# Issuing the cache copies of a hybrid decoder step from ScalarE

## The chip, the core and the metric

The kernel runs on one core of a Trainium2 chip. The core has a matrix engine (TensorE, PE in the profile, with its weight loads as PEld), VectorE (DVE), ScalarE (ACT), GpSimd (POOL) and SyncE (SP), which here only issues transfers. Sixteen DMA engines move data between DRAM and the on-chip memory, and from DRAM to DRAM. The metric is the device time of one launch in microseconds (us).

## What is computed

One decoder layer for a prompt of 512 tokens and for 8 samples of 4 new tokens, all in float32:

```python
h = rms_norm(x, norm_pre)
z = einsum('btd,de->bte', h, w_in)              # 2048 -> 7680: q | k | v | gate | conv a, b | conv gate
att = dilated sliding-window attention, 12 heads # samples read the cache of 2048 old K/V rows
c   = conv module over 512 channels
y = einsum('bte,ed->btd', concat(att * silu(g_att), c * silu(g_conv)), w_out)
x + rms_norm(y, norm_post)
kv_s.append(concatenate([buf, kvs], axis=1)[:, kvs.shape[1]:])   # new cache: old rows moved up by 4
```

The last line matters here. The new cache of each sample is its old cache without the first 4 rows, then the 4 new rows. So 8 times 2044 rows of 12,288 bytes, 201 MB, are copied from DRAM to DRAM unchanged.

## The kernel before

**Projection.** TensorE multiplies w_in with all 544 tokens in 60 projections of 128 output columns, each in four chunks of 512 rows. Both factors are split into a high and a low part of a faster type. A weight chunk is loaded into a tile `raw` (half of a projection's weights, 512 KB, four buffers), ScalarE casts it to `wh` (line 809), GpSimd subtracts to get `wl` (line 810), and then TensorE uses both. A cast is put into the program two chunks ahead of its use, a load two halves ahead of the cast. Projections 0 to 2 run together at the start (`project_first`), and the inverse norms are made at their end; projection 3 is the first of the steady run.

**Beside it.** Attention of the prompt, the samples' attention (which loads the old cache as `kvf` and `kvm`) and the convolution are generators. `tick`, called after each half of two chunks, lets each go on by a step. So every engine's instructions stand in the order in which this one Python program writes them, and `in_order` pins that order.

**Output projection.** From about 957 us on TensorE multiplies with w_out (`owh`, `owl`, `oz`); the samples' rows use `raw` itself (`os`).

**Transfers.** All 635 loads, stores and copies go through `dma` (line 98), which issues from SP. The copies are 176 pieces of 96 rows (1152 KB; 8 of them 336 KB). At its end each `tick` calls `bulk(START + PACE * pe[0])`, which issues copies until the bytes sent by all transfers reach a number that grows with the matmul columns written so far. The framework gives the transfers eight completion semaphores, DMAHW0 to DMAHW7, in turn over the whole program, whichever engine issues them. Before a transfer takes a semaphore again, its issuer waits until the transfer that had it last has landed.

Of the kernel before, what the change touches and what calls it, by code (L numbers as in the profile page):

```python
# [30 lines left out]
ROW = 2 * NH * P  # L31
# [54 lines left out]
def body(tc, xT, xtok, gpost, w_in, w_out, ckv, cconv, relb, vecs, pww, c_oht, c_ohr, c_lmr, c_tm, c_pick,  # L86
         o_y, o_kvp, o_cp, o_cs, o_kvs):
    nc = tc.nc
# [5 lines left out]
    sent = [0]  # L94

    def dma(out, in_):
        sent[0] += 4 * math.prod(out.shape)
        return tc.keep_in_program_order(nc.sync.dma_start(out, in_))
# [222 lines left out]
    def bulk(upto):  # L321
        while d2d_at[0] < len(d2d) and sent[0] < upto:
            b, r, n = d2d[d2d_at[0]]
            d2d_at[0] += 1
            s = ckv[b, NT + r:NT + r + n].rearrange("r c -> (r c)").rearrange("(e x) -> e x", e=16)
            o = o_kvs[b, r:r + n].rearrange("r c -> (r c)").rearrange("(e x) -> e x", e=16)
            dma(o, s)

# [436 lines left out]
    def tick():  # L767
        for s in sorted(sides, key=lambda s: s.rank):
            s.advance(now[0])
            if s.over:  # L770
                sides.remove(s)
        now[0] += 1
        t = now[0]
        flush_late(t)
        bulk(START + PACE * pe[0])
# [370 lines left out]
    for c in range(4):  # L1146
        last = c == 3

        for bs in (((0, 1), (2,), (3,)) if last else ((0, 1), (2, 3))):
# [22 lines left out]
            if last:  # L1172
                if 0 in bs:

                    nc.scalar.activation(stat[:, 0, 8:9], epsc, AF.Sqrt)
                for b in bs:
                    finish(b)
                if 0 in bs:
                    load_xt(2)
                    load_xt(3)  # L1180
                    finish(4)
                if 2 in bs:
                    bulk(1 << 60)
# [116 lines left out]
```

## Time and profile before

| | |
|---|---|
| median of 3 runs | 1174.95 us (1173.05 to 1175.88) |
| the profiled execution | 1170.97 us |
| its span, first to last instruction | 1169.2 us |
| mean granted TensorE clock | 0.99 |
| TensorE busy | 1137.5 us, 97% |
| ScalarE busy | 378.1 us, 32% |
| bytes moved by DMA | 401.92 MB, 344 GB/s over the span |

An engine is busy while it computes; waiting and issuing a transfer do not count. The idle time that matters is that of the engine on which the others wait; that of the rest costs nothing.

### The profile page before, as it was taken

Reading aid. Unit: us, or ns where it says so; the run is one execution under the profiler, and the core shown is the slowest. Engines: PE = TensorE matmul, PEld = TensorE weight load, DVE = VectorE, ACT = ScalarE, POOL = GpSimd, SP = SyncE. Lnnn points to the kernel's source line nnn. Section 1 sums busy time; section 2 is a strip of 40 time slices with the busy share of each in tenths; the row PEclk is TensorE's granted clock in tenths of the full one; section 3 lists DMA queues with packets and bytes.
Section 4 is the critical chain, followed back from the end, with each engine's and each line's share of the span. In section 5 each row is a group of like instructions: output and inputs, shape, how many; then the busy total and the mean of one; then the engine's idle time right before and its main releaser. Section 6 shows DMA issues by size and latency. Waiting matters only on the chain.

```text
span 1169.2 us, 23598 instructions
## 1 busy us (share of the span) xinstructions
PE 1137.5 (97%) x9322; PEld 1029.4 (88%) x9322; DVE 674.0 (58%) x1997; ACT 378.1 (32%) x749; POOL 406.8 (35%) x353
## 2 busy tenths in 40 slices
PE   7899999999999999999999999999999999999996
PEld 7699999999999999999999999899999976776775
DVE  5209899599699988778233576994222243112136
ACT  5433333422123332331334333423222253223241
POOL 5043323344344333333322222334333445313130
PEclk9989999999999999999999999999999998999999
DMA  9899999999998998999998899889999968999966
GB/s 363 278 339 373 402 351 343 383 312 338 408 329 320 402 381 323 351 362 355 408 375 331 293 384 395 330 317 373 387 386 338 337 218 292 337 357 389 332 232 225
DMA packets 96083, 401.92 MB, mean 344 GB/s; under 512 B 15000, under 2 KB 17816, under 8 KB 89765
## 3 DMA queue, kind: packets, MB, share of 16 engines
q1 hardware_dynamic: 95972, 400.42, 93.6%
q8 instruction: 73, 1.20, 0.4%
q14 instruction: 38, 0.30, 0.1%
HBM read 388.65 MB, written 212.66 MB: 514 GB/s over the span
## 4 chain that ended last, share of the span: by engine, by line
PE 56%; DVE 2%; DMA 1%; issue 1%; POOL 0%; ACT 0%; SPq 0%; DVEq 0%; ACTq 0%; POOLq 0%
PE z L107 32%; PE oz L107 14%; PE o L109 3%; PE pwp L107 1%; PE os L109 1%; PE att L107 1%; DMA raw<-in_w_out_dram 1%; PE s L107 1%; PE t L113 1%; DVE qsc L628 1%; POOL owl L844 0%; PE kt L113 0%; PE pvar L107 0%; PE pm L107 0%; PE sn L109 0%
## 5 line engine op out<-in xcount | busy, mean ns | idle before, releaser
L107 PE MATMUL z<-xh,wh 128*128 128x272 f32 x1920 | 572.3, 298 | 8.7 <-ACT wh L894 7.6
L107 PE MATMUL z<-xh,wl 128*128 128x272 f32 x1920 | 555.0, 289 | 1.1 <-POOL wl L895 0.6
L107 PE MATMUL z<-xl,wh 128*128 128x272 f32 x1920 | 553.4, 288 | 0.0
L810 POOL TENSOR_TENSOR wl<-raw,wh 128x512 fp32r<-128x512 f32 x228 | 311.1, 1374 | 471.3 <-ACT wh L809 447.7
L107 PEld LDWEIGHTS z<-xh,wh 128*128 128x128 f32 x1920 | 363.6, 189 | 25.2 <-issue 11.0
L107 PEld LDWEIGHTS z<-xl,wh 128*128 128x128 f32 x1920 | 363.2, 189 | 1.6 <-issue 1.0
L107 PEld LDWEIGHTS z<-xh,wl 128*128 128x128 f32 x1920 | 363.0, 189 | 1.8 <-POOL wl L895 0.9
L809 ACT CAST wh<-raw 128x512 fp32r<-128x512 f32 x228 | 139.1, 617 | 181.4 <-PE z L107 106.4
L334 DVE TENSOR_TENSOR t<-z,R 128x272 f32<-128x272 f32 x96 | 42.0, 439 | 181.5 <-PE z L107 170.2
L628 DVE SCALAR_TENSOR_TENSOR qsc<-kvf,qb 128x128 f32<-128x128 f32 x288 | 125.6, 436 | 8.8
L628 DVE SCALAR_TENSOR_TENSOR qsc<-kvm,qb 128x128 f32<-128x128 f32 x288 | 112.4, 390 | 8.8
L442 DVE SCALAR_TENSOR_TENSOR mix<-up,vec,mix 128x512 f32<-128x512 f32 x120 | 107.6, 896 | 0.0
L107 PE MATMUL oz<-owl,mh 128*128 128x512 f32 x256 | 101.7, 397 | 3.7 <-POOL owl L844 3.7
L107 PE MATMUL oz<-owh,mh 128*128 128x512 f32 x256 | 103.4, 404 | 1.5 <-ACT owh L843 1.5
L107 PE MATMUL oz<-owh,ml 128*128 128x512 f32 x256 | 101.3, 396 | 0.0
L844 POOL TENSOR_TENSOR owl<-raw,owh 128x512 fp32r<-128x512 f32 x43 | 61.4, 1447 | 111.2 <-ACT owh L843 81.8
L107 PEld LDWEIGHTS oz<-owh,mh 128*128 128x128 f32 x256 | 48.5, 189 | 26.4 <-issue 8.4
L844 DVE TENSOR_TENSOR owl<-raw,owh 128x512 fp32r<-128x512 f32 x21 | 21.7, 1032 | 73.0 <-ACT owh L843 72.8
L107 PEld LDWEIGHTS oz<-owl,mh 128*128 128x128 f32 x256 | 48.7, 190 | 15.6 <-POOL owl L844 4.1
L843 ACT CAST owh<-raw 128x512 fp32r<-128x512 f32 x64 | 36.8, 618 | 78.3 <-DMA raw<-in_w_out_dram 69.4
L107 PEld LDWEIGHTS oz<-owh,ml 128*128 128x128 f32 x256 | 48.4, 189 | 10.6
L444 DVE SCALAR_TENSOR_TENSOR mix<-us,vec,mix 128x32 f32<-128x32 f32 x120 | 57.0, 475 | 0.0
(180 smaller groups left out, 991.7 us busy)
## 6 DMA issues: line engine op xcount, KB each, us to landing
out_dram<-in_ckv_dram SPq DMA_DIRECT2D x168, 1152.0 KB, 12.2
raw<-in_w_in_dram SPq DMA_DIRECT2D x119, 512.0 KB, 9.7
kvm<-in_ckv_dram SPq DMA_DIRECT2D x48, 1024.0 KB, 10.5
kvf<-in_ckv_dram SPq DMA_DIRECT2D x144, 256.0 KB, 8.2
raw<-in_w_out_dram SPq DMA_DIRECT2D x32, 512.0 KB, 9.1
out_dram<-t SPq DMA_DIRECT2D x24, 256.0 KB, 9.2
mix<-in_xtok_dram SPq DMA_DIRECT2D x4, 1024.0 KB, 14.0
xt<-in_xtok_dram SPq DMA_DIRECT2D x8, 512.0 KB, 4.7
```

The source lines that it names most:

```text
L107: nc.tensor.matmul(out, lhsT, rhs, start=start, stop=stop)
L109: nc.tensor.matmul(out, lhsT, rhs, start=start, stop=stop, tile_position=tile_position)
L113: nc.tensor.transpose(out, in_, eye)
L334: nc.vector.tensor_tensor(dst[:, sl], z[hf][:, :HT], R[:, sl], op=ALU.mult)
L442: nc.vector.scalar_tensor_tensor(cc[:, ct, :SEQ], up[:, j:j + SEQ], wj, cc[:, ct, :SEQ], op0=ALU.mult, op1=ALU.add)
L444: nc.vector.scalar_tensor_tensor(cs, us[:, :, j:j + NT], wj, cs, op0=ALU.mult, op1=ALU.add)
L628: nc.vector.scalar_tensor_tensor(scr, src[:, hh * P:hh * P + P], SCALE, qb[:, hh * P:hh * P + P], op0=ALU.mult, op1=ALU.mult, accum_out=sd ...
L809: nc.scalar.copy(wh, raw)
L810: nc.gpsimd.tensor_tensor(wl, raw, wh.bitcast(F32), op=ALU.subtract)
L843: nc.scalar.copy(wh, raw)
L844: (nc.vector if j % 3 == 2 else nc.gpsimd).tensor_tensor(wl, raw, wh.bitcast(F32), op=ALU.subtract)
```

## The change

The copies no longer go through `dma`. `bulk` counts their bytes itself and issues them from ScalarE, into ScalarE's own hardware queue. Where they stand in the program, their number, sizes and the pacing are the same, and so are all loads and stores.

```diff
@@ -324,7 +324,8 @@
             d2d_at[0] += 1
             s = ckv[b, NT + r:NT + r + n].rearrange("r c -> (r c)").rearrange("(e x) -> e x", e=16)
             o = o_kvs[b, r:r + n].rearrange("r c -> (r c)").rearrange("(e x) -> e x", e=16)
-            dma(o, s)
+            sent[0] += 4 * n * ROW
+            tc.keep_in_program_order(nc.scalar.dma_start(o, s))
```

**First place: ScalarE between the tables and projection 3.** `base` is the last table; `wh12` is the first cast of projection 3. Before:

```order
L309 COPY base_80<-rb_609 96x512 [waits PE_49]
L309 COPY base_80<-rb_612 96x416 [waits PE_49]
L809 CAST wh12_632<-raw6_138 128x512 [waits DMAHW5_49]
L809 CAST wh13_636<-raw6_138 128x512 [waits Pool_49]
L809 CAST wh14_642<-raw7_140 128x512 [waits DMAHW6_49,Pool_49]
```

Now:

```order
L309 COPY base_80<-rb_609 96x512 [waits PE_49]
L309 COPY base_80<-rb_612 96x416 [waits PE_49]
L328 DMA out_4_dram<-in_ckv_dram 32x9216 [waits DMAHW4_49]
L328 DMA out_4_dram<-in_ckv_dram 32x9216 [waits DMAHW2_49]
L328 DMA out_4_dram<-in_ckv_dram 32x9216 [waits DMAHW3_49]
L328 DMA out_4_dram<-in_ckv_dram 32x9216 [waits DMAHW4_49]
L810 CAST wh12_632<-raw6_138 128x512 [waits DMAHW5_49]
```

Four copies now stand between the last table and the first cast. The first and the fourth wait for the same semaphore: the fourth's wait is for the landing of the first.

**The same place on SP.** `dtab` stores a table, `kvf0` is the first load of old cache rows. Before:

```order
L98 DMA mix1_87<-in_xtok_dram 32x2048 [waits DMAHW1_49,Activation_49]
L98 DMA out_4_dram<-in_ckv_dram 32x9216 [waits DMAHW2_49]
L98 DMA out_4_dram<-in_ckv_dram 32x9216 [waits DMAHW3_49]
L98 DMA out_4_dram<-in_ckv_dram 32x9216 [waits DMAHW4_49]
L98 DMA out_4_dram<-in_ckv_dram 32x9216 [waits DMAHW5_49]
L98 DMA dtab_79<-tabs_102 12x640 [waits DMAHW6_49,Activation_49]
```

Now:

```order
L98 DMA mix1_87<-in_xtok_dram 32x2048 [waits DMAHW1_49,Activation_49]
L98 DMA dtab_79<-tabs_102 12x640 [waits DMAHW2_49,Activation_49]
L98 DMA kvf0_624<-in_ckv_dram 128x1x512 [waits DMAHW3_49,DMAHW2_49,DMAHW4_49,DMAHW0_49,DMAHW5_49,DVE_49,PE_49]
L98 DMA kvf0_624<-in_ckv_dram 128x1x512
L98 DMA kvf0_624<-in_ckv_dram 128x1x512 [waits DMAHW6_49]
```

The four copies have left SP, where they stood ahead of the table's store. The second copy on ScalarE waits for `dtab` to land (DMAHW2) and the third for the first `kvf0` (DMAHW3).

**Second place: ScalarE around projections 14 and 15**, now (before, the same rows without the four transfers):

```order
L696 COPY spt0_2760<-sn0_937 32x128
L328 DMA out_4_dram<-in_ckv_dram 32x9216 [waits DMAHW7_49]
L810 CAST wh59_2827<-raw29_2574 128x512 [waits Pool_49]
L328 DMA out_4_dram<-in_ckv_dram 32x9216 [waits DMAHW0_49]
L810 CAST wh60_2887<-raw30_2676 128x512 [waits DMAHW6_49,PE_49,Pool_49]
L328 DMA out_4_dram<-in_ckv_dram 32x9216 [waits DMAHW7_49]
L810 CAST wh61_2923<-raw30_2676 128x512 [waits PE_49,Pool_49]
L561 COPY vtm0_2952<-tmv0_2861 32x512 [waits PE_49]
L328 DMA out_4_dram<-in_ckv_dram 32x9216 [waits DMAHW0_49]
L810 CAST wh62_2987<-raw31_2781 128x512 [waits DMAHW2_49,PE_49,Pool_49]
```

Of the four copies the third waits for the landing of the first (DMAHW7), and the fourth for that of the second (DMAHW0), with casts behind each.

## Rows read from the trace of the kernel before

**Rows 1.** The page, busy us of each engine, share of span, instructions.

```profile
PE 1137.5 (97%) x9322; PEld 1029.4 (88%) x9322; DVE 674.0 (58%) x1997; ACT 378.1 (32%) x749; POOL 406.8 (35%) x353
```

**Rows 2.** What TensorE waited for: us in total, times, longest.

```profile
PE z L107 <- ACT wh L894: 7.6, 1, 7.6
PE oz L107 <- POOL owl L844: 3.7, 1, 3.7
PE rbx L107 <- DVE diagx L208: 3.3, 1, 3.3
...
PE oz L107 <- ACT owh L843: 1.5, 1, 1.5
PE z L107 <- ACT wh L809: 1.1, 1, 1.1
...
PE os L109 <- DMA raw<-in_w_out_dram: 0.2, 1, 0.2
```

**Rows 3.** Stretches: length, busy by engine (instructions), PE clock, DMA share, GB/s.

```profile
60.00:460.00 400.00, 398.75 (x3540) 378.75 (x3538) 325.42 (x1054) 126.36 (x260) 150.72 (x139) 0.99 0.99 360
460.00:730.00 270.00, 270.00 (x2436) 251.70 (x2436) 157.95 (x502) 92.09 (x194) 86.79 (x80) 1.00 0.98 360
```

**Rows 4.** The copies' issues on SP: duration ns min/median/max, first and last start.

```profile
L98 SPq DMA_DIRECT2D out_dram<-in_ckv_dram x176: 509/580/2842, 39.2 to 1117.0; - x176
```

**Rows 5.** What SP's queue waited for: us in total, times, longest.

```profile
SPq L98 <- DMA out_dram<-in_ckv_dram: 93.1, 46, 3.6
```

**Rows 6.** SP from 36 to 76 us: start, us, instruction, count.

```profile
39.19 3.46 SPq L98 DMA_DIRECT2D out_dram<-in_ckv_dram  x4
54.20 0.33 SPq L98 DMA_DIRECT2D dtab<-tabs  x1
58.34 1.92 SPq L98 DMA_DIRECT2D kvf<-in_ckv_dram  x3
60.30 0.60 SPq L98 DMA_DIRECT2D kvm<-in_ckv_dram  x1
60.95 1.52 SPq L98 DMA_DIRECT2D raw<-in_w_in_dram  x3
```

**Rows 7.** ScalarE from 40 to 78 us: start, us, instruction [idle before].

```profile
58.35 0.50 ACT L309 COPY base<-rb 96x416 f32<-96x416 f32 x1 [1.79 <-PE rb L107]
58.75 2.17 ACT L809 CAST wh<-raw 128x512 fp32r<-128x512 f32 x4
```

**Rows 8.** The four copies issued from 39 to 43 us, start to landing.

```profile
DMA to landing us min/median/max: 7.4/9.0/10.6
```

**Rows 9.** The page, DMA issues: count, KB each, median us to landing.

```profile
out_dram<-in_ckv_dram SPq DMA_DIRECT2D x168, 1152.0 KB, 12.2
...
xt<-in_xtok_dram SPq DMA_DIRECT2D x8, 512.0 KB, 4.7
```

**Rows 10.** All transfers to outputs in the whole span, start to landing.

```profile
DMA to landing us min/median/max: 2.1/11.6/26.0
```

**Rows 11.** Stretches around two TensorE pauses, columns as in rows 3.

```profile
54.00:59.40 5.40, 3.41 (x4) 0.64 (x4) 0.00 (x0) 1.81 (x5) 0.00 (x0) 0.55 0.14 55
59.40:64.80 5.40, 4.86 (x20) 4.54 (x21) 0.00 (x0) 1.52 (x3) 4.97 (x4) 0.50 0.84 266
...
965.90:972.70 6.80, 5.28 (x15) 2.53 (x16) 3.63 (x3) 1.97 (x4) 6.80 (x5) 0.50 0.37 114
```

**Rows 12.** ScalarE from 224 to 256 us.

```profile
234.36 0.25 ACT L695 COPY spt<-sn 32x128 f32<-32x128 f32 x1
...
236.52 0.62 ACT L809 CAST wh<-raw 128x512 fp32r<-128x512 f32 x1 [1.39 <-issue]
238.03 0.62 ACT L809 CAST wh<-raw 128x512 fp32r<-128x512 f32 x1 [0.89 <-PE z L107]
```

**Rows 13.** SP from 219 to 256 us.

```profile
221.44 1.15 SPq L98 DMA_DIRECT2D out_dram<-in_ckv_dram  x2
...
227.76 1.51 SPq L98 DMA_DIRECT2D out_dram<-in_ckv_dram  x2
```

**Rows 14.** TensorE: the first matmul that uses the cast of 238.03 us.

```profile
249.25 0.28 PE L107 MATMUL z<-xh,wh 128*128 128x272 f32 x1
```

**Rows 15.** The page: GpSimd's subtraction that follows each cast.

```profile
L810 POOL TENSOR_TENSOR wl<-raw,wh 128x512 fp32r<-128x512 f32 x228 | 311.1, 1374 | 471.3 <-ACT wh L809 447.7
```

## The prediction

> **What bounds the kernel now.** I read the busy time of each engine first: TensorE is busy 1137.5 of 1169.2 us, ScalarE a third of the span [rows 1]. Then the stretches: in the 670 us from 60 to 730 us TensorE is busy 398.75 of 400 and 270.00 of 270 us [rows 3]. So the steady run is bound by TensorE, and whatever holds up TensorE there is added to the end in full. Then what TensorE waited for: the reader is to see that no wait of note goes back to a transfer, the only one being 0.2 us [rows 2]. The DMA engines are as full as TensorE (share 0.98 to 0.99, 360 GB/s [rows 3]), but their work runs ahead of it.
>
> A shorter load therefore has next to nothing to win. What can be lost is large: ScalarE casts every weight chunk that TensorE uses, and the copies now stand in its queue.
>
> **What leaves SP.** 176 issues of 0.58 us, 102 us [rows 4], and the waits of SP for a copy to land, 93.1 us [rows 5]. No engine on the path waits for SP, so I count 0. If the cover went, the saving could not exceed the two waits of TensorE at the start of the output projection, 3.7 + 1.5 = 5.2 us [rows 2], where casts and their subtractions follow loads of w_out.
>
> **What comes onto ScalarE: issuing.** The same 102 us of issues. ScalarE's busy time of 378.1 becomes about 480 of 1169 us; spread over the run, one issue of 0.58 us in front of a cast is hidden, since a cast is done far ahead: the one of 238.03 us [rows 12] is first used at 249.25 us [rows 14]. It needs 0.62 us itself and 1.37 us for GpSimd's subtraction [rows 15], so it may start as late as 249.25 - 1.37 - 0.62 = 247.26 us: 9.2 us of slack. I count 0 for the bare issues there.
>
> **What comes onto ScalarE: the waits.** A copy waits in ScalarE's queue until the transfer that last had its semaphore has landed, and every cast behind it waits too. SP reaches its copies early: it issued the two pairs of the second place at 221.44 and 227.76 us [rows 13], while ScalarE comes to those places only behind its instructions of 234.36 and 236.52 us [rows 12]. Most semaphores are free by then. Two kinds of places remain.
>
> *First place, the start of projection 3.* SP issued the four copies at 39.19 us [rows 6], when ScalarE was still squaring tokens, and the DMA engines had little else. Now they stand between `base`, which ends at 58.35 + 0.50 = 58.85 us, and the cast of 58.75 us [rows 7] for which TensorE is already waiting (the 1.1 us in [rows 2]). There is no slack here. Step by step: copy 1 is issued at 58.85 us. Copy 2 needs `dtab`, stored at 54.20 us [rows 6], free. Copy 3 needs the first `kvf`, issued at 58.34 us [rows 6]; it lands before copy 1. Copy 4 needs copy 1's landing. How long does that take? The first and fastest of the four took 7.4 us with nothing behind it [rows 8]; the median of all is 12.2, and 512 KB late in the kernel took 4.7 us [rows 9]. Copy 1 shares the DMA engines with seven loads of SP issued from 58.34 to 62.5 us [rows 6]. I take 9.0 us, the median of the four [rows 8]. So copy 4 is issued at 58.85 + 9.0 = 67.85 us, takes 0.58 us, and the cast starts at 68.43 instead of 58.75 us: **+9.7 us**. Ends: with 4.7 us it is +5.4, with 12.2 us +12.9.
>
> *The clock after that pause.* The granted clock was 0.50 from 59.4 to 64.8 us [rows 11], the lower of its levels (1.2 instead of 2.4 GHz), after TensorE had been busy only 3.41 of the 5.4 us before; in those 5.4 us half the work was lost, 2.7 us. After the pause at 961 to 967 us it was 0.50 for 6.8 us [rows 11], 3.4 us lost. With a pause three times as long in the first place I take the second price in place of the first: **+0.7 us**. Ends: -2.7 (full clock by the time TensorE starts) and +2.4 (some 10 us at half clock, as the first two of those rows together, which is 5.1 lost).
>
> *Dense places in the steady run.* Where two copies that stand close together on ScalarE are eight transfers apart, the second waits for the whole flight of the first. At the second place copy A is issued at 234.61 us (234.36 + 0.25 [rows 12]). With the median flight of 12.2 us [rows 9] it lands at 246.81; copy C waits for it, is issued, and the cast behind it starts at 247.4 instead of 238.03 us. Its limit was 247.26, so TensorE loses 0.1 us: the slack is just used up. With a longer flight the excess goes to the end one for one. Two queues now share the DMA engines, so a longer flight is possible; the longest of all output transfers before took 26.0 us [rows 10]. At 19 us, halfway, the cast starts at 234.61 + 19 + 0.58 = 254.2 us and 6.9 us are lost. The order has three such stretches, around 240, 510 and 710 us. So this term lies between 0 (3 x 0.1) and 21 us (3 x 6.9). I take **+5 us**, near the lower end, since 12.2 is a median of 168 flights and 26.0 the end of one tail.
>
> *The end.* The last copy was issued at 1117.0 us [rows 4], over 50 us before the span ends; a copy that comes 10 to 20 us later still lands in time. 0.
>
> **Sum.** 0 + 0 + 9.7 + 0.7 + 5 + 0 = 15.4 us. The span of 1169.2 becomes 1184.6 us, the profiled execution's 1170.97 becomes 1186.4. The median of the runs shown is 4.0 above that execution, so on it I forecast 1174.95 + 15.4 = **1190.4, say 1190 us**, slower. Own range: low 5.4 - 2.7 + 0 = +2.7, 1178; high 12.9 + 2.4 + 21 = +36, 1211, which already contains the next case.
>
> **Rivals.** *A, the waits spread.* The flights become long because both queues are full, and all three dense stretches pay in full: 9.7 + 0.7 + 21 = 31.4, 1206 us. It decides from the point where a flight exceeds 247.26 - 0.58 - 234.61 = 12.1 us by several us. For it: a DMA share of 0.99 [rows 3] and a median at that very limit. Against it: SP's loads lose the copies in front of them, so the transfers for which ScalarE waits may land sooner.
>
> *B, no difference.* Copy 1 lands in 4.7 us, the clock is full when TensorE starts (-2.7), and the 5.2 us of the output projection's start go, because w_out is no longer queued behind copies: 5.4 - 2.7 - 5.2 = -2.5; with the 9.0 us flight +1.8. About 1175 us. For it: the DMA engines were idle at 54 to 59 us (share 0.14 [rows 11]). Against it: each of three terms has to fall to its end.
> The rows show SP losing 93.1 us to waits for copies [rows 5] without TensorE noticing. The Trainium skill, "DMA: Bandwidth & Descriptors", section "Issuing engines are not separate DMA queues", says that transfers issued by different engines run on the same 16 DMA engines and interleave, and that issuing from several saves only the sequencer's time. By that rule alone the change would be worth nothing, 1175 us, and it speaks against any gain from a second queue; it is silent on what the wait does to the engine that now issues. The trace agrees so far as no wait of TensorE goes back to SP.
>
> *C, faster.* The change does what a second queue could at best: loads pass the copies, the four copies at the start are issued without a wait, and TensorE's 5.2 us at the output projection vanish: 1169.8 us. It decides only if the fourth copy doesn't wait for the first, which its semaphore in the order speaks against.
>
> **Chances.** Forecast 0.62, A 0.19, B 0.13, C 0.06. The range of 8 in 10 is 1178 to 1210: the forecast's own, and most of A. A measurement of this kernel tells about 0.3% (3.5 us) from no change. Faster by more: 0.06 (C). Within: 0.13 (B). Slower: 0.81 (forecast and A).
>
> **What would show it.** In the profile of the changed kernel: (1) a gap on TensorE of about 10 us more before projection 3, ended by the cast of line 810, and ScalarE waiting there for a copy; if the cast comes by 61 us, the first term is wrong. (2) The clock at 0.50 for some 7 us after it. (3) TensorE's waits for that cast between 240 and 260 us, near 520 and near 720 us; none means term three is 0, over 20 us in sum means A. (4) ScalarE busy for no longer, but its queue waiting for transfers; SP's waits for copies smaller or moved. If TensorE waits for loads instead (`raw`, `kvf`), because SP's transfers wait for semaphores that late copies hold, the reason is wrong though the sign may be right.

## The result and the profile after

The change makes the kernel slower: 1210.88 us in the median (1209.74 to 1212.8, four runs) against 1174.51, ratio 1.0311, 95% interval 1.0293 to 1.0329. The forecast was 1190 us and its range ended at 1210. The sign was right and the loss, 36.4 us, is more than twice the 15.4 that were counted.

The page of the changed kernel: busy time (answers to [rows 1]), then the DMA queues (queue, packets, MB, share of the 16 engines' span), then the issues (answer to [rows 9]: count, KB each, median us to landing).

```profile
PE 1151.3 (95%) x9322; PEld 1036.7 (86%) x9322; DVE 668.5 (55%) x1997; ACT 379.2 (31%) x749; POOL 405.0 (33%) x353
...
q1 hardware_dynamic: 87652, 199.47, 47.7%
q10 hardware_dynamic: 8320, 200.94, 45.2%
...
out_dram<-in_ckv_dram ACTq DMA_DIRECT2D x168, 1152.0 KB, 8.9
...
raw<-in_w_out_dram SPq DMA_DIRECT2D x32, 512.0 KB, 14.5
```

The change did what it says: half of the bytes went through a queue of ScalarE's own, q10. ScalarE is no busier, and the copies themselves fly shorter than before (8.9 against 12.2 us); the loads of w_out fly longer. (The page's medians are over those transfers whose landing it could assign. Over all of them, from the semaphores in the trace, the copies flew 8.9 us in the median, 11.9 before, and the 32 loads of w_out 10.7 us, 8.0 before.) Even so TensorE, with the same instructions, ends 41 us later. What it waited for (answers to [rows 2]: us in total, times, longest):

```profile
PE z L107 <- ACT wh L810: 12.2, 4, 8.2
PE z L107 <- ACT wh L895: 8.1, 1, 8.1
PE os L109 <- DMA raw<-in_w_out_dram: 5.7, 5, 2.5
PE oz L107 <- POOL owl L845: 4.9, 1, 4.9
PE t L113 <- ACT pt L377: 4.3, 2, 4.1
```

ScalarE's casts (12.2 instead of 1.1, of it 8.2 before projection 3), one of its COPY instructions in the steady run (`pt`), and now loads of w_out (5.7 instead of 0.2). To see where the time goes I compared the start of TensorE's first matmul of each projection in the two traces. After minus before, stretch by stretch, of the span's 40.9 us: 1.4 until `base`; 7.0 in the pause before projection 3; 4.8 from there to projection 5; 3.3 to projection 41 (680 us); **11.4** from 41 to 46 (784 us); -0.5 to 59 (969 us); **13.4** from there to the end.

**First place.** ScalarE (start, us, instruction, idle before and what ended it; answers to [rows 7]), then SP:

```profile
59.75 0.50 ACT L309 COPY base<-rb 96x416 f32<-96x416 f32 x1 [1.79 <-PE rb L107]
59.76 7.40 ACTq L328 DMA_DIRECT2D out_dram<-in_ckv_dram  x4
67.20 2.18 ACT L810 CAST wh<-raw 128x512 fp32r<-128x512 f32 x4 [6.95 <-DMA out_dram<-in_ckv_dram]
...
62.42 25.47 SPq L98 DMA_DIRECT2D raw<-in_w_in_dram  x5
```

Four issues take 7.4 us because the fourth waits for the first copy to land (issued at 59.76, landed at 66.6 us), and the cast stands behind them. The second row lies beside `base`, not after it: an issue runs while the engine still computes. TensorE's clock meanwhile (stretch, length, busy PE, PEld, DVE, ACT, POOL, PE clock, DMA share, GB/s; answers to [rows 11]):

```profile
56.90:74.00 17.10, 7.74 (x26) 5.67 (x26) 0.00 (x0) 3.26 (x6) 4.97 (x4) 0.50 0.81 267
...
995.60:1005.80 10.20, 5.98 (x17) 3.09 (x18) 3.05 (x5) 3.43 (x8) 9.69 (x6) 0.50 0.38 120
```

It is at the lower of its levels, 1.2 GHz, for 17.1 us around the pause, and for 10.2 us at the start of the output projection, where it was 6.8 us before.

**Steady run, near 690 and 763 us.** ScalarE:

```profile
690.61 0.52 ACTq L328 DMA_DIRECT2D out_dram<-in_ckv_dram  x1
691.22 0.62 ACT L810 CAST wh<-raw 128x512 fp32r<-128x512 f32 x1 [8.52 <-DMA out_dram<-t]
...
763.17 0.52 ACTq L328 DMA_DIRECT2D out_dram<-in_ckv_dram  x1
763.73 0.62 ACT L810 CAST wh<-raw 128x512 fp32r<-128x512 f32 x1 [8.54 <-DMA kvm<-in_ckv_dram]
```

In both a copy is issued at the moment at which the earlier transfer of SP on its semaphore lands (690.6 and 763.2 us), and a cast comes right behind it. The transfer waited for is not a copy: a store of attention rows (`out_dram<-t`, 12.9 us in flight) and a load of old rows (`kvm`, 14.2 us).

**Output projection.** From the chain that ended last, its loads of w_out (start, us, what):

```profile
962.80 20.42 DMA raw<-in_w_out_dram
...
1041.12 12.97 DMA raw<-in_w_out_dram
1062.49 28.56 DMA raw<-in_w_out_dram
1094.36 13.83 DMA raw<-in_w_out_dram
...
1147.23 13.90 DMA raw<-in_w_out_dram
```

Five loads of 512 KB that fly 13 to 29 us are on the path; the kernel before has one there, of 11.6 us. (The longest, `raw139`, flew 23.6 us before as well, and no wait of TensorE went back to it.) They are issued no later than before: `raw120` 31 us ahead of the first product with w_out (before: 29 us), and when it was issued 135 copies had been issued, 136 before. The flight itself is longer.

### The profile page after: what moved, and what is told of

It reads as the page before. It is cut to its first block, busy times and chain, and to the rows that moved or that the text cites. A ratio compares the mean times of both kernels' runs of the same rounds, so it can differ in the third digit from the quotient of the medians.

```text
span 1210.1 us, 23580 instructions
## 1 busy us (share of the span) xinstructions
PE 1151.3 (95%) x9322; PEld 1036.7 (86%) x9322; DVE 668.5 (55%) x1997; ACT 379.2 (31%) x749; POOL 405.0 (33%) x353
## 4 chain that ended last, share of the span: by engine, by line
PE 43%; DMA 12%; issue 2%; POOL 1%; DVE 1%; ACT 0%; SPq 0%; ACTq 0%; DVEq 0%; POOLq 0%
PE z L107 25%; PE oz L107 10%; DMA raw<-in_w_out_dram 7%; PE o L109 3%; DMA raw<-in_w_in_dram 2%; DMA out_dram<-t 2%; DMA kvm<-in_ckv_dram 1%; PE os L109 1%; POOL wl L811 1%; PE att L107 1%; PE s L107 1%; PE pwp L107 1%; POOL owl L845 0%; PE t L113 0%; PE pvar L107 0%
## 5 line engine op out<-in xcount | busy, mean ns | idle before, releaser
L107 PE MATMUL z<-xh,wh 128*128 128x272 f32 x1920 | 574.9, 299 | 20.2 <-ACT wh L810 12.2
L107 PEld LDWEIGHTS z<-xh,wh 128*128 128x128 f32 x1920 | 365.8, 191 | 37.7 <-ACT wh L810 14.9
L629 DVE SCALAR_TENSOR_TENSOR qsc<-kvf,qb 128x128 f32<-128x128 f32 x288 | 120.7, 419 | 8.8
L629 DVE SCALAR_TENSOR_TENSOR qsc<-kvm,qb 128x128 f32<-128x128 f32 x288 | 109.5, 380 | 8.7
L443 DVE SCALAR_TENSOR_TENSOR mix<-up,vec,mix 128x512 f32<-128x512 f32 x120 | 102.9, 857 | 0.0
L445 DVE SCALAR_TENSOR_TENSOR mix<-us,vec,mix 128x32 f32<-128x32 f32 x120 | 59.9, 499 | 0.0
L844 ACT CAST owh<-raw 128x512 fp32r<-128x512 f32 x64 | 36.4, 617 | 71.6 <-DMA raw<-in_w_out_dram 44.2
L107 PEld LDWEIGHTS oz<-owh,ml 128*128 128x128 f32 x256 | 48.8, 190 | 10.8 <-DVE ml L788 0.2
(180 smaller groups left out, 1000.1 us busy)
## 6 DMA issues: line engine op xcount, KB each, us to landing
kvf<-in_ckv_dram SPq DMA_DIRECT2D x144, 256.0 KB, 10.2
mix<-in_xtok_dram SPq DMA_DIRECT2D x4, 1024.0 KB, 13.1
```

The lines of the kernel that those rows point to most:

```text
L107: nc.tensor.matmul(out, lhsT, rhs, start=start, stop=stop)
L443: nc.vector.scalar_tensor_tensor(cc[:, ct, :SEQ], up[:, j:j + SEQ], wj, cc[:, ct, :SEQ], op0=ALU.mult, op1=ALU.add)
L445: nc.vector.scalar_tensor_tensor(cs, us[:, :, j:j + NT], wj, cs, op0=ALU.mult, op1=ALU.add)
L629: nc.vector.scalar_tensor_tensor(scr, src[:, hh * P:hh * P + P], SCALE, qb[:, hh * P:hh * P + P], op0=ALU.mult, op1=ALU.mult, accum_out=sd ...
L844: nc.scalar.copy(wh, raw)
```

## The experiments

Theory 1 is the prediction's: a copy waits on ScalarE for the transfer that had its semaphore, and holds the casts. Theory 2 came from the last fence: between two queues the DMA engines take turns by pieces, so that large pieces in one queue hold up small ones in the other. A piece is one packet record of the trace. In the changed kernel: a copy goes in pieces of 36,864 bytes (5376 of them, median 1.41 us on one DMA engine), a w_in or w_out load in pieces of 4096 bytes (0.159 us), `kvf`, `kvm` and stores in pieces of 2048 (0.084 us). (The "some 24 KB" in an expectation below is the mean of all records of q10, and 2816 of these are semaphore increments of 4 bytes.) In one queue a load waits only for what was issued ahead of it; between two, large pieces issued later could pass it. The rivals: a backlog of copies that moves from place to place; plain shortage of DMA throughput.

The stretches are cut from the profiled execution as above, minus those of the kernel before, in us; the kernel before had 1173.4 to 1174.5 us beside them.

| kernel | median us | ratio, 95% interval | to `base` | pause before 3 | 3-5 | 5-41 | 41-46 | 46-59 | 59-end |
|---|---|---|---|---|---|---|---|---|---|
| changed | 1210.9 | 1.029-1.033 | 1.4 | 7.0 | 4.8 | 3.3 | 11.4 | -0.5 | 13.4 |
| first4_sp | 1196.3 | 1.016-1.022 | -0.1 | 0.0 | 0.0 | 1.7 | 8.5 | -0.1 | 10.8 |
| dense_sp | 1197.7 | 1.018-1.024 | 1.2 | 7.0 | 2.8 | 2.3 | 0.0 | 5.2 | 8.1 |
| tail_sp | 1198.2 | 1.019-1.023 | 0.5 | 11.7 | 0.2 | 1.2 | 12.1 | -0.1 | 1.2 |
| places_sp | 1179.9 | 1.003-1.007 | 4.4 | 0.0 | 0.9 | 1.9 | 0.0 | 3.4 | 1.3 |
| copies_pool | 1196.5 | 1.018-1.021 | 14.3 | 0.0 | 0.8 | 2.0 | 0.0 | 2.1 | 6.3 |
| small_act | 1217.4 | 1.036-1.040 | -0.5 | 8.3 | -0.3 | 20.8 | 13.5 | -0.1 | 0.1 |
| small_sp | 1215.6 | 1.034-1.039 | 0.5 | 0.0 | 0.7 | 15.3 | 3.0 | 6.7 | 17.0 |
| rows12_act | 1239.7 | 1.052-1.059 | -1.1 | 7.8 | 2.9 | 32.0 | 17.7 | -0.6 | 9.9 |
| rows12_sp | 1211.2 | 1.030-1.033 | 2.3 | 0.0 | -0.4 | 14.0 | 1.7 | 5.1 | 17.5 |
| tail_small | 1191.4 | 1.014-1.018 | -0.2 | 7.0 | 3.1 | 2.7 | 9.8 | -0.1 | -1.1 |
| dense_small | 1207.2 | 1.026-1.031 | 0.6 | 7.1 | 2.8 | 1.1 | 12.1 | -0.1 | 15.3 |
| after_pw2k | 1202.4 | 1.022-1.026 | 3.2 | 7.5 | 2.2 | 2.0 | 8.2 | -0.1 | 7.8 |
| dense_small_pw2k | 1209.9 | 1.028-1.033 | 2.1 | 7.1 | 2.9 | 1.3 | 15.1 | -0.1 | 13.4 |
| tail_act | 1180.0 | 1.003-1.007 | 0.8 | 0.0 | 0.6 | 0.0 | 0.0 | 1.0 | 6.7 |
| tail_act_small | 1172.7 | 0.998-1.001 | -0.5 | 0.0 | 0.3 | 0.0 | 0.0 | 0.0 | 0.1 |
| **small16_act** | 1183.0 | 1.006-1.009 | 2.2 | 7.0 | 0.4 | 0.0 | 2.7 | -0.1 | 0.0 |
| small16_sp | 1174.4 | 0.999-1.002 | 2.0 | 0.0 | 0.6 | 0.0 | 0.0 | 0.0 | 1.0 |
| tail_act_small16 | 1172.2 | 0.998-1.000 | 2.1 | 0.0 | -0.5 | 0.0 | 0.0 | 0.0 | -1.4 |

### Where: three places put back one by one

```diff
-            tc.keep_in_program_order(nc.scalar.dma_start(o, s))
+            eng = nc.sync if d2d_at[0] <= 4 else nc.scalar          # first4_sp
+            eng = nc.sync if 88 < d2d_at[0] <= 109 else nc.scalar   # dense_sp
+            eng = nc.sync if d2d_at[0] > 130 else nc.scalar         # tail_sp
+            tc.keep_in_program_order(eng.dma_start(o, s))
```

places_sp has all three conditions together.

> The first four copies go through SP again, as before the change; the other 172 stay on ScalarE. Theory 1 (a copy on ScalarE waits for an earlier transfer and holds the casts behind it; the first place is one such place and its loss goes to the end): the pause of TensorE before projection 3 falls from 8.2 us to about 1 us, the clock after it is as before, and the time is 1210.9 - 13.3 = about 1198 us. Rival (the run is short of DMA throughput, and what is gained early is lost again later): projection 5 starts 13 us earlier, but the end comes less than 6 us earlier, 1205 us or more.

> Copies 89 to 109 of 176, those that ScalarE issued between about 660 and 800 us, go through SP; all others stay on ScalarE. Theory 1: the two steps of +5.7 us (projection 42) and +5.8 us (projection 46) come from casts behind copies that wait in ScalarE's queue at these places; without them about 1210.9 - 11.5 = 1199 us. If the two steps only show a backlog of copies that has built up since the start: 1206 us or more, with steps at other projections.

> The first 130 copies stay on ScalarE; the last 46, those that ScalarE issued from 941 us on, go through SP in the old order. If the 13.4 us lost in the output projection come from copies being issued by ScalarE at that place: about 1197 us, with the flights of the w_out loads back from 14.5 to about 9 us in the median. If they come from a backlog that was there before the output projection began (the copies already late by then), the time stays above 1205 us.

> The first 4 copies, copies 89 to 109 and the last 46 go through SP; the other 105 stay on ScalarE in rows of 36 KB. If the three places account for the loss and are independent: 1210.9 - 14.6 - 11.5 - 12.7 = 1172 us by the single runs, and with the 2.8 us that were lost elsewhere in the steady run 1172 to 1178 us. If the places feed each other or the loss only moves to the next place: 1183 us or more.

Each takes its own stretch to zero or close, 14.6, 13.2 and 12.7 us by the medians. The other stretches keep most of their loss, but not the same: with tail_sp the pause grew from 7.0 to 11.7 us, and with dense_sp a new step of 5.3 us came at projection 51, behind a copy that waited for a `kvm` load (8.3 us of idle ScalarE). Together they leave 6 us, 2 more than the upper end expected; the profile shows most of that ahead of `base` and between 46 and 59, of it 3.5 us at projection 51 again. So the losses are mainly local and no backlog, though a small part moves on to the next such place. With first4_sp the cast starts right behind `base`:

```profile
58.21 0.50 ACT L309 COPY base<-rb 96x416 f32<-96x416 f32 x1 [1.79 <-PE rb L107]
58.61 2.17 ACT L811 CAST wh<-raw 128x512 fp32r<-128x512 f32 x4
```

These runs tell where, not why: each takes the wait and the second queue away at once.

### Taking the waits away, keeping the second queue

```diff
-            tc.keep_in_program_order(nc.scalar.dma_start(o, s))
+            tc.keep_in_program_order(nc.gpsimd.dma_start(o, s))
```

> The copies are issued by GpSimd into its queue, in the same places of the program, rows of 36 KB. There they have completion semaphores of their own, so a copy waits at most for the eighth copy before it, and ScalarE's casts stand behind no copy. Theory 1 alone: the waits are gone and with them the 40 us: 1175 us, plus what issuing costs GpSimd (not known from the runs so far; up to 5 us if its subtractions come later at the places where TensorE waits for them). Theory 2: the first place loses nothing, but the w_out loads still fly about 14 us beside the copies and the output projection still loses about 11 us, with 2 to 6 us at 690 us: 1186 to 1195 us.

No cast stands behind a copy now, and the pause and the stretch 41 to 46 are at zero, as theory 1 has it. But the output projection still loses 6.3 us. In its first bunch there, eight copies issued between 994.9 and 1000.1 us, two w_out loads issued at 998 us flew 17.4 and 29.5 us. A new loss of 14.3 us comes before `base`: nothing holds the first four copies back any more, they go out from 30.9 us on instead of 39.2, small loads of SP beside them fly 16 to 22 us, SP issues the tokens' last load `mix` at 50.9 instead of 38.8 us, and ScalarE waits for it (16.2 us, before 3.5):

```profile
ACT mix L273 <- DMA mix<-in_xtok_dram: 16.2, 1, 16.2
```

### Smaller pieces

small_act and small_sp cut the copies into rows of 4 KB, rows12_act and rows12_sp into rows of 12 KB:

```diff
-            s = ....rearrange("(e x) -> e x", e=16)
+            s = ....rearrange("(g e x) -> e g x", g=4, x=1024)   # small: 72 x 4 rows; rows12: x=3072, 24 x 4 rows
```

> All copies stay on ScalarE and move the same bytes at the same places, but each is cut into rows of 4 KB instead of 36 KB, so that its pieces are no larger than those of a load. Theory 2 (the two queues take turns at the DMA engines piece by piece, so that a load's pieces of some 2 KB wait behind copy pieces of some 24 KB, and loads that fly beside copies are slow): the flights of the w_out loads fall from 14.5 to about 9 us in the median, the output projection loses at most 3 instead of 13.4 us, the steady run some less too: 1200 us or less. Theory 1 alone (only the waits of the copies in ScalarE's queue matter): the copies take as long as before or longer, the waits stay, about 1211 us or more.

> The kernel before with copies cut into rows of 4 KB: the control for small_act. If rows of 4 KB cost nothing of themselves: 1175 us, with a median flight of the copies of about 12 us. If the DMA engines move such rows more slowly, the copies' flights grow, SP waits longer and the time rises; then small_act must be read against this one and not against the kernel before.

> All copies on ScalarE, cut into rows of 12 KB: pieces about half as large as before, still several times those of the loads. Theory 2: the w_out loads fly some 11 us in the median, and the output projection loses 4 to 8 instead of 11.2 us; about 1204 us. Theory 1 alone: no change, 1211 us.

> The kernel before with copies in rows of 12 KB, the control for rows12_act. If pieces of 12 KB move as fast as the larger ones: 1175 us. If they cost throughput as rows of 4 KB did (1215.6 us on SP), the time lies between 1175 and 1215 us, and rows12_act is to be read against it.

The controls on SP lost 38 to 41 us by themselves, so the totals tell nothing of the change. The reason is in the increments with which the DMA engines report a transfer as landed: 2816 for the 176 copies of the changed kernel, 16 each, but 2072 here, 168 times 12 and 8 times 7. A copy ran on 12 of the 16 DMA engines. That agrees with the Trainium skill, "DMA: Bandwidth & Descriptors", section "Why a DMA increments its semaphore by 16 and not by 1", by which a transfer is spread over the largest number up to 16 that divides its outermost dimension (72 and 24 give 12). Pieces cost nothing by themselves: 0.159 us for 4096 bytes is the rate of 1.41 us for 36,864.

Still, at 12 engines each, rows of 12 KB on ScalarE lost 9.9 us in the output projection and rows of 4 KB 0.1 (their controls 17.5 and 17.0). I then used 4 KB rows at one place at a time.

> All copies on ScalarE; only the last 46, those of the output projection, are cut into rows of 4 KB, the first 130 keep their rows of 36 KB. Theory 2 (between two queues the DMA engines share by pieces, so small pieces of loads starve beside large pieces of copies): the w_out loads no longer fly 14.5 us in the median but about 9, and the stretch from the first product with w_out to the end loses at most 3 instead of 11.2 us against the kernel before: 1200 to 1203 us. Theory 1 alone (the copies' waits in ScalarE's queue): rows of 4 KB move more slowly, the copies land later, the waits stay or grow: 1211 us or more.

> All copies on ScalarE; the same 21 copies (89 to 109) in rows of 4 KB, so each waits for the same semaphore as in the changed kernel. Theory 2 (a transfer of SP flies long because large pieces of copies in the other queue take its turns, and the copy that waits for that transfer waits as long): the store before the cast at 690 us and the kvm load before the one at 763 us, which flew 12.9 and 14.2 us, fly under 9 us, the two steps of together 11.5 us shrink to 5 or less: about 1204 us. Theory 1 without 2 (the waits come from transfers that are issued late, not from long flights): the steps stay, 1209 us or more.

> The first 130 copies through SP as before the change, the 46 of the output projection through ScalarE in their old rows of 36 KB: the same as tail_act_small (1172.7 us) but for the size of the rows, and no copy is late when the output projection begins. Theory 2 (large pieces in the other queue overtake the w_out loads): 11 to 13 us are lost there, 1184 to 1188 us, with flights of w_out loads of 17 us and more beside copies. If the loss in the changed kernel needed the copies that were late from before: within 3 us of 1173 us.

tail_act_small is tail_act with the 46 copies in rows of 4 KB.

> The first 130 copies go through SP as before the change, only the 46 of the output projection through ScalarE, in rows of 4 KB. Theory 2: with small pieces the second queue costs nothing there, 1172 to 1176 us, beside 1187 us if ScalarE's queue itself costs the 11 to 13 us of the output projection whatever the pieces. Under 1171 us it would beat the kernel before.

In the output projection theory 2 holds: with the first 130 copies on SP, nothing late and nothing else changed, large pieces cost 6 us in the median and small ones nothing. The 6 are half of what was expected; in the kernels with large pieces on ScalarE this stretch lost between 6.7 and 15.3 us, and what sets the size I did not find. Near 690 us theory 2 seemed to fail: in dense_small the store still flew 12.1 us, and the step of 6.2 stayed. One reading was that the `pw` load ahead of the store, with pieces of 512 bytes, starves even beside 4 KB:

```diff
-            dma(pw, pww[:, :, n * P:(n + 1) * P])
+            dma(pw, pww[:, n, :].rearrange("p (c e) -> p c e", c=4))
```

> The changed kernel, but the four loads of pw read pieces of 2 KB instead of 512 bytes (the weights are laid out so in DRAM; same bytes, same places, same semaphores). Theory 2 in the steady run (the pw load ahead of the store has the smallest pieces of all, so it starves most beside copies, the store behind it in SP's queue lands late, and the copy that waits for that store holds the cast at 690 us): the flight of the pw load there falls from 13.0 to about 5 us, the store lands some 6 us earlier, and the step of +5.7 us at projection 42 goes: about 1205 us. If the flights there are long because so many transfers start together, whatever their pieces: no change, 1208 to 1213 us.

> dense_small with the same change to pw: beside copies in rows of 4 KB no transfer of SP has pieces under 2 KB there. Theory 2: the step of +6.2 us at projection 42, which small copy rows alone did not remove, goes: about 1201 us against 1207.2. If so many transfers started together are the cause: the step stays, 1205 us or more.

The `pw` load did fly 6.0 instead of 13.0 us, but the step at projection 42 stayed in both (6.2 and 9.2 us), so that reading is out. The run after_pw2k is 8.5 us faster than the changed kernel all the same, in the later stretches. In the second, the store landed in 8.3 us and ScalarE then stood at the next copy, one that waits for another copy. ScalarE in dense_small_pw2k:

```profile
682.75 0.80 ACTq L330 DMA_DIRECT2D out_dram<-in_ckv_dram  x1
683.65 0.62 ACT L812 CAST wh<-raw 128x512 fp32r<-128x512 f32 x1 [4.02 <-PE z L107]
...
692.54 0.81 ACTq L330 DMA_DIRECT2D out_dram<-in_ckv_dram  x1
693.47 0.62 ACT L812 CAST wh<-raw 128x512 fp32r<-128x512 f32 x1 [7.85 <-DMA out_dram<-in_ckv_dram]
```

The copy it waited for ran on 12 engines and flew 17.6 us. So the experiment had a fault of its own, the 12 engines, and the next one takes it out. Whether that fault alone kept the step in dense_small is not shown: no run has small rows on 16 engines for these 21 copies only.

### Smaller pieces on all 16 DMA engines

```diff
+            g, e, x = (9, 32, 1024) if n == 96 else (7, 16, 768)
+            s = ....rearrange("(g e x) -> e g x", g=g, x=x)      # 32 x 9 rows of 4 KB
```

> small_act once more, but with the rows of 4 KB arranged so that each copy runs on all 16 DMA engines; in the traces of small_act and small_sp a copy's completion was counted by 12 of them (2072 increments of 168 copies of 12 and 8 of 7, where the kernel before has 16 for each). Theory 2 for the output projection, theory 1 for the rest: the output projection loses under 2 us, the pause before projection 3 and the steps near 690 and 763 us stay, 1210.9 - 13.4 = about 1197 us. If not the size of the pieces but the four engines left free made the w_out loads fast in small_act: about 1211 us, with 8 us or more lost in the output projection.

> The control: the kernel before with these rows of 4 KB on 16 DMA engines. If the 41 us that small_sp lost came from the 12 engines: 1175 us. If rows of 4 KB cost throughput of themselves: 1200 us or more.

> tail_act_small with its 46 copies on all 16 DMA engines. Size of the pieces decides: 1172 to 1175 us, as before, with flights of the w_out loads under 12 us. If the free engines decided in tail_act_small: about 1180 us as in tail_act.

The control is at 1174.4 us, no different from the kernel before, so the 12 engines were what cost 41 us. With all copies on ScalarE, same places and same semaphores, the kernel now takes 1183.0 us, 14 better than expected: not only the output projection is at zero, but also nearly all of the steady run. The queues of small16_act, and its first place:

```profile
q1 hardware_dynamic: 87652, 199.47, 46.7%
q10 hardware_dynamic: 52096, 200.94, 46.4%
...
60.59 7.37 ACTq L330 DMA_DIRECT2D out_dram<-in_ckv_dram  x4
68.00 2.18 ACT L812 CAST wh<-raw 128x512 fp32r<-128x512 f32 x4 [6.91 <-DMA kvf<-in_ckv_dram]
...
678.88 0.58 ACTq L330 DMA_DIRECT2D out_dram<-in_ckv_dram  x1
679.55 0.62 ACT L812 CAST wh<-raw 128x512 fp32r<-128x512 f32 x1 [3.84 <-PE z L107]
```

The pause of 7 us before projection 3 is there as before: that wait does not depend on the size of the pieces. (The view names a `kvf` load, which landed at 68.25 us, after the cast had begun. The fourth copy was issued at 67.38 us, and the first one, on the same semaphore, had landed at 67.36.) Near 690 us the copy still waits for the store, but the store lands in 8.2 instead of 12.9 us, and the cast comes in time. Who passes whom, from issues and landings in the traces, over the 32 w_out loads of each kernel: how often a copy issued after a load lands before it, how often a load lands before a copy issued ahead of it; then the flights of five loads that TensorE or a cast waited for in the changed kernel, in us.

```
                      before  changed  tail_act  small16_act  tail_act_small16
copy passes load         0       16        8          0             0
load passes copy         0        0        0         22            23
flights over 12 us       6       14       12          0             0
raw120                  7.2     20.3     12.7        9.9          11.4
raw121                  5.3     20.4     16.1        8.1           7.5
raw122                 10.3     19.1     18.2        8.4           7.6
raw140                  6.4     14.9     14.7        8.1           8.6
raw148                  6.2     13.1     12.6        7.6           8.5
```

In one queue nothing passes. Beside a second queue with large pieces copies pass the loads; with small pieces the loads pass the copies. The six long flights of before (23 to 27 us, behind six or seven copies) are of loads that are not needed soon, since the order issues copies and loads together there; no wait of TensorE goes back to them. What the samples' product `os`, which uses `raw` directly, and its weight loads waited for (idle us, times), changed kernel, tail_act and tail_sp (before: 1.3; in small16_act and tail_act_small16 no such row):

```profile
  DMA raw<-in_w_out_dram: 16.3, 12
```

```profile
  DMA raw<-in_w_out_dram: 14.1, 12
```

```profile
  DMA raw<-in_w_out_dram: 1.5, 2
```

tail_act_small16 has 1172.2 us, 0.9989 of the kernel before, interval 0.9979 to 0.9999. That lies inside the 0.3% that a measurement here tells from no change, so nothing was found that beats both kernels. small16_act with its first four copies on SP was not run.

## Why the prediction was wrong

The step that failed is the last term, *The end*, set at 0 for a reason that does not bear on it: 13.4 us were lost there. The term for the dense places was too small as well, 5 for 14.2 us. The pause in the first place was foreseen.

**First place: the mechanism right, the size close.** The fourth copy waited for the first and held the cast. Copy 1 flew 6.9 us where 9.0 was taken, so the cast came at 67.20 instead of 68.43 us, 8.5 us later than before where 9.7 was counted. Of that 7.0 us are the pause; `base` itself came 1.4 later in this execution. first4_sp took all of it away. The 9.0 is no median of four flights: the view of [rows 8] could assign two landings, 7.4 and 10.6 us, and by the semaphores the four flew 7.4, 10.6, 13.5 and 16.0 (the 12.2 us of [rows 9] is likewise over a part of the copies). That the first `kvf` lands before copy 1 was true here (it flew 3.3 us) and not in tail_sp, where it flew 10.8 us, the third copy waited for it and the pause was 11.7 us. So the place can cost more than the prediction's single path allows.

**The clock after it: small, as counted; the stretch lost more for another reason.** 0.7 us was counted; from projection 3 to 5 the changed kernel lost 4.8. Of that 2.5 us are TensorE's waits at 83 to 86 us for casts whose load `raw8` flew 21.8 us (7.9 before), and after these waits the granted clock fell a second time, to 0.50 for 3.4 us (87.6 to 91.0), at most 1.7 us of lost work. The first fall, 17.1 us, lay mostly over the pause itself: TensorE worked at 1.2 GHz for about 6 us after it, and for 5.4 us before the change. small16_act had the same pause and the same 17.1 us, no such waits and no second fall, and lost 0.4 there.

**Dense places: the term was 5, the measured 14.2, and the places were wrong.** The prediction looked for two *copies* eight transfers apart (240, 510, 710 us). No step shows there; near 690 and 763 us the copy waited for a *store* and a *load* of SP. Their flights were taken as unchanged or shorter. small16_act shows the rest: with equal pieces the wait remains in the program and costs 2.7 instead of 11.4 us.

**The end: the step that failed.** It asked only whether the last copies land in time, and counted 0. That was true and beside the point: 13.4 us were lost there because loads of w_out flew long beside the copies. In that stretch TensorE's waits sum to 13.4 us (5.7, 4.9 and 2.8), to 5.4 before, and it was at 1.2 GHz for 10.2 and 3.4 us where it had been for 6.8 (leaving out the last 8 us of either kernel). Taking only the 46 copies of this stretch off ScalarE brought the loss to 1.2 us (tail_sp), and cutting all copies into 4 KB pieces brought it to 0.0 (small16_act). The argument had it the wrong way round in the case against rival A: "SP's loads lose the copies in front of them, so the transfers for which ScalarE waits may land sooner". They no longer had copies in front of them in their queue, but beside them: from 953 to 984 us, while `raw120` to `raw122` flew, the copies' queue had 0.67 of the DMA engines' time and SP's 0.24. The fourth of the signs named TensorE's waits for loads, but as its cause semaphores that late copies hold; these loads were issued in time and flew long.

**SP's relief and the bare issues: 0, right.** TensorE's two waits at the start of the output projection did not shrink (4.9 and 2.8 us after). ScalarE's busy time stayed at 379 us, and not 480: an issue does not count as busy and ran beside a computing instruction at 59.76 us.

**The rivals.** A (1206 us) came nearest, and that flights become long is half of what happened; but it put the whole price into three stretches of the steady run, and the flights that grew were SP's (w_out loads), while the copies' fell to 8.9 us. B's case drew on the Trainium skill, "DMA: Bandwidth & Descriptors", section "Issuing engines are not separate DMA queues": transfers of different engines interleave on the same 16 DMA engines, and only the issue is saved. I read that as "no difference"; the trace agrees with the interleaving, and with pieces of 36 KB the interleaving is what cost most. The Trainium skill says on that page, section "Queues, rings and completion order", that a DMA engine takes turns between queues packet by packet; the runs agree in kind, since the size of the pieces alone moved 1210.9 to 1183.0 us.

By the runs, then: 36.4 us lost, of which 28 go away when the pieces of 36 KB are cut to 4 KB (1210.9 to 1183.0), and the rest, 8.5 to 9.6 us by the two values of the kernel before, is mostly the wait at the first place (7.0 in the profile).

## What to carry to other kernels

The second DMA queue was here not only a second place to issue from: it removed the order between its transfers and the others, and with pieces nine times as large as those of the loads in the first queue it slowed these loads where they were urgent. Look at the bytes per piece on both sides before splitting queues, cut the background copy into rows as small as the loads', and count by the increments whether it still runs on all 16 DMA engines (here with 32 outermost rows, and not with 72 or 24). A transfer issued from an engine that computes puts the wait for its semaphore into that engine's queue (7 us of TensorE before projection 3), so look at what transfer of *any* queue held the semaphore before, not only at transfers of the same kind.

## What was not expected of the hardware

- **Shares between two queues depend on the size of the pieces.** If turns were strictly one piece each, a w_out load (128 pieces, 8 on each DMA engine) beside a full queue of copies would take 8 x (1.41 + 0.16) = 12.6 us, an estimate from the records' medians; `raw140` and `raw148` flew 14.9 and 13.1. But a `kvm` load (512 pieces of 2048 bytes, 32 each) would take 48 us by this, and flew 14.2. What a turn holds stays open.
- **12 of 16.** Copies in SP's one queue with rows arranged 72 x 4 (4 KB) or 24 x 4 (12 KB), on 12 DMA engines, cost 41 and 38 us; arranged 32 x 9 (4 KB), on 16, nothing.
- **In one queue the size of the pieces cost nothing.** Copies in pieces of 4096 instead of 36,864 bytes in SP's one queue: 1174.4 us, ratio 0.999 to 1.002.
- **An issue runs beside a computing instruction** of its engine (at 59.76 us within the 0.50 us of `base`; some 125 of the 176 issues of 0.52 us overlap one). In small16_act, between projections 5 and 41, some 85 of them on ScalarE cost 0.0 us.
